# Shift and scale of the first norm as matrix products in 32-column strips, two tiles ahead of the query products

## The chip, the cores and the metric

The kernel runs on one core of a Trainium2 chip. The metric is the time of one execution on the device, in microseconds; lower is better. PE is TensorE (PEld its weight loads), DVE is VectorE, ACT is ScalarE, POOL is GpSimd, SP is SyncE, which issues most of the transfers.

## The reference

A two-part network runs on 256 tokens of width 1024: a transformer of two layers and a second block with a state-space branch, a pooling branch and 64 routed experts. The change is in the first thing that the first layer does. Two condition vectors, `c` for the tokens and `c_ctx` for 256 context tokens, go through silu and a matrix; out of the 6144 results the first 1024 are a shift, the next 1024 a scale. The normalised tokens are scaled and shifted by them, feature by feature, and then projected to queries, keys and values.

```python
def rmsnorm(x, g):
    return x * lax.rsqrt(jnp.mean(x * x, axis=-1, keepdims=True) + RMS_EPS) * g
...
silu_c, silu_cc = jax.nn.silu(c), jax.nn.silu(c_ctx)[None, :]
mod = (silu_c @ ada_w[i] + ada_b[i])[:, None, :]
mod_c = (silu_cc @ ada_w[i] + ada_b[i])[:, None, :]
sh1, sc1, g1, sh2, sc2, g2 = jnp.split(mod, 6, axis=-1)
h = rmsnorm(x, norm1_g[i]) * (1.0 + sc1) + sh1        # and hc from ctx, csh1, csc1
q, k, v = jnp.split(h @ wqkv, 3, axis=-1)             # keys and values from hc, too
```

## The kernel before

The activations lie with features on the 128 partitions: `x` is 8 tiles of 128 features by 256 tokens, and so are `ctx` (`cx`) and what is made of them. The order of every engine's instructions is the order of the Python program (`tc.manual_schedule()`); a helper inserts the semaphores.

Weights of the projections come through `Stream`: each piece `st` is 1 MB and holds two units of eight 128x128 blocks, in a ring of 4 buffers. `raw()` (L162) hands a unit over as it is, in fp32; `split_to` (L134) splits a unit into a high part `wh` (ACT, L143) and a low part `wl` (DVE, L131), which later products use in three cheaper passes (`mm3`, L274). The query products use raw units, unit n against tile n, and sum over the eight tiles in four PSUM buffers `ps_q`; so all eight tiles have to be normalised one after another, and the key products begin when the last is done.

The stage of the change runs from the start to the key products (L524 to L627). First the mean squares of `x` are formed (`sums`, L546: a square on ACT and an add on DVE per tile; `total`, L557; `row_rstd`, L565: a chain of tiny DVE operations and two products that spread the result over the partitions, `rows`). Then, for each of the eight tiles n:

- `coefs_x(n, j)` (L497): the weights of this tile's 128 shifts (j = 0) and 128 scales (j = 1) are `AW[n]`, 1 MB, with one output feature per partition. `ada_unit` (L388, L390) multiplies 1024 of its columns with `crow[:, 0]`, which is silu(c) spread over all partitions, and sums them, in one DVE operation of 128x1024.
- `coefs_c(n)` and `sum_c(n)` (L503, L508): the same for the context, by a POOL product with `crow[:, 1]` (L506) and an ACT sum (L511).
- `finish_x` (L482) and `finish_c` (L488) add bias and gain, in `ab`; `modulate` (L513) makes `na` (DVE, L516), `full` and `hH` (ACT, L519, L520) and the rest `hL` (DVE, L521).
- eight query products of 128x256 in fp32 (L617).

The program writes the coefficients of tile n+1 between the two halves of tile n's modulation, and the query products at the end of the turn. `AW` has four buffers, borrowed from `kT` and `v`; `load_a(n + 4)` (L474) reuses a buffer when its products are done. SP's queue is in program order, so a load that waits for a buffer holds the loads behind it.

In the key stage that follows, DVE also works off a background list: two products of 128x1024 with `crow` per weight unit (`ada`, L390), for the later layers' coefficients.

Of the kernel before, what the change touches and what calls it, by code (L numbers as in the profile page):

```python
# [8 lines left out]
F32 = mybir.dt.float32  # L9
# [8 lines left out]
P = 128  # L18
# [22 lines left out]
_off = 0  # L41
for _n, _w in (("ident", 128), ("tri", 128), ("cos", 256), ("sin", 256), ("pinv", 64)):
    CST[_n] = (_off, _w)
    _off += _w
NCST = _off


# [57 lines left out]
class Stream:  # L105
# [56 lines left out]
    def raw(self):  # L162

        u = self.pos // 8
        w = self.slots[u // 2][:, u % 2].rearrange("p (a c) -> p a c", a=8)
        if u % 2:
            del self.slots[u // 2]
        self.pos += 8
        self.nu = u + 1
        return w  # L170
# [249 lines left out]
def build(ctx, tc, ap):  # L420
# [14 lines left out]
    b.vecs = cp.tile([P, NVEC], F32, name="vecs")  # L435
    nc.scalar.dma_start(b.csts[:, :P], ap["csts"][:, :P])
    nc.scalar.dma_start(b.vecs[:, :VHEAD], ap["vecs"][:, :VHEAD])
# [13 lines left out]
    L0 = ExitStack()  # L451
    lp = L0.enter_context(tc.tile_pool(name="l0", bufs=1))
    qT = lp.tile([P, 8, T], F32, name="qT")
    kT = lp.tile([P, 8, 2, T], F32, name="kT")
# [19 lines left out]
    def load_a(n):  # L474
        AW[n] = spare[n % 4]
        nc.sync.dma_start(AW[n], ap["ada0s"][n])
# [16 lines left out]

    raw = cp.tile([P, KD, 4], F32, name="ada_raw")
    prods = {}
# [31 lines left out]
    st.limit = 0  # L527
    nc.sync.dma_start(crow[:, 0], ap["c"].to_broadcast([P, D]))
# [3 lines left out]
    nc.sync.dma_start(crow[:, 1], ap["c_ctx"].to_broadcast([P, D]))  # L532
    load_w()
    load_a(1)
    for i in range(2):
        nc.sync.dma_start(cxs[i], ap["ctx"][:, 4 * i:4 * i + 4])
    load_a(2)
    load_w()
    load_a(3)
    xs = [x[:, k] for k in ks]  # L540
    nc.scalar.activation(crow[:, 0], crow[:, 0], AF.Silu)
    nc.vector.scalar_tensor_tensor(bsc, b.vecs[:, ab + 8:ab + 16], 1.0, b.vecs[:, n1:n1 + 8], op0=ALU.add, op1=ALU.mult)
    ms = b.aux.tile([P, 512], F32, tag="aux", name="ms")
    rps = b.aux.tile([P, 512], F32, tag="aux", name="rows")

# [25 lines left out]

    total(0, sums(xs))
    row_rstd(0)
    coefs_x(0, 0)
    coefs_x(0, 1)
    nc.scalar.activation(crow[:, 1], crow[:, 1], AF.Silu)
    rows_x, rows_c = rps[:, :T], rps[:, T:]
    coefs_c(0)
    psq = [b.ps.tile([P, 2, T], F32, tag="ps", name="ps_q") for _ in range(4)]
    ready = []  # L580
    for n in ks:
        full = b.wk.tile([P, T], F32, tag="rp_b", name="full", bufs=2)
        todo = [modulate(xs, rows_x, n, 0, full)]
        next(todo[0])
        if n == 1:
            total(1, sums(cx))
        if n == 2:
            row_rstd(1)
        if n + 1 < KD:
            coefs_x(n + 1, 0)  # L590
        if n >= 2:
            for i in ready:
                finish_c(i)
                todo.append(modulate(cx, rows_c, i, 1))
                next(todo[-1])
            ready = []
        for o in todo:
            next(o)
        if n + 1 < KD:
            coefs_x(n + 1, 1)  # L600
        sum_c(n)
        ready.append(n)
        if n + 1 < KD:
            coefs_c(n + 1)
        if n + 4 < KD:
            load_a(n + 4)
        if n in (1, 3, 4):
            load_w()
        if n == 4:
            for t_, o in ((b.csts, "csts"), (b.vecs, "vecs")):  # L610
                c0 = P if o == "csts" else VHEAD
                nc.scalar.dma_start(t_[:, c0:], ap[o][:, c0:])
        w = st.raw()
        if n == KD - 1:
            st.more(1)
        for i in range(KD):
            nc.tensor.matmul(psq[i // 2][:, i % 2], lhsT=w[:, i], rhs=full, start=(n == 0 and i % 2 == 0), stop=(n == KD - 1),  # L617
                             skip_group_check=True)
    st.limit = st.n
    finish_c(KD - 1)  # L620
    mc_ = modulate(cx, rows_c, KD - 1, 1)
    next(mc_)
    nc.scalar.activation(qT[:, 0:2], psq[0], AF.Copy)
    next(mc_)
# [4 lines left out]
    nc.scalar.dma_start(crow[:, 1], ap["c_2"].to_broadcast([P, D]))  # L629
    b.ada_bufs = [b.adap.tile([P, D], F32, name=f"ada{i}") for i in range(2)]  # L630
# [1043 lines left out]
    ex.give(x.rearrange("p k t -> p (k t)"))  # L1674
    spare = [wr.rearrange("p k e -> p (k e)")] + [b.csts[:, P + i * T:P + (i + 1) * T] for i in range(2)]
    us = mw.tile([P, 2, 512], F32, tag="oH", name="u", bufs=1)
# [409 lines left out]
def layout(i):  # L2086
# [31 lines left out]
    o, w = CST["ident"]  # L2118
    cst[:, o:o + w] = np.eye(P)
    o, w = CST["tri"]  # L2120
    cst[:, o:o + w] = np.triu(np.ones((P, P)))
# [20 lines left out]
    out["c"] = f("c").reshape(1, D)  # L2142
    out["c_ctx"] = f("c_ctx").reshape(1, D)
    out["c_2"] = f("c_2").reshape(1, D)
    ada = f("ada_w")
    out["ada0s"] = np.ascontiguousarray(ada[0][:, :2 * D].reshape(D, 2, KD, P).transpose(2, 3, 1, 0)).reshape(KD, P, 2048)
    out["ada0"] = np.ascontiguousarray(ada[0][:, 2 * D:].T).reshape(32, P, D)
# [79 lines left out]
```

## Time and profile before

| | |
|---|---|
| median of 3 runs | 1622.66 us (1619.64 to 1630.2) |
| the profiled execution, its own time | 1618.75 us |
| its span in the profile | 1616.9 us |
| key products begin at | 84.38 us of the span |
| busy over the span: PE, DVE, ACT, POOL | 93%, 64%, 42%, 20% |

A query product in fp32 shows as two PE records, since the engine takes it in two passes; so eight of them are 16 records. A row of the timeline that joins several instructions gives the time from the first one's start to the last one's end. Records of pipelined matmuls overlap: the time that one costs is the distance to the next one's start.

### The profile page before, as it was taken

How to read it: one execution, taken by the hardware profiler on the slowest of the kernel's cores; microseconds unless marked ns; L12 is line 12 of the kernel's file. 1: busy time of each engine (PE TensorE's matmuls, PEld its weight loads, DVE VectorE, ACT ScalarE, POOL GpSimd, SP SyncE). 2: the span in 40 equal slices, each digit the busy share in tenths (PEclk: the TensorE clock that was granted, in tenths of full speed). 3: DMA queues.
4: the chain of work that ended last, by engine and by line, in shares of the span. 5: the costliest groups of instructions: out<-in, count | busy, mean ns of one | idle time of the engine just before them, and what ended most of it. 6: DMA issues, size and time to landing. Idle time of an engine off the chain costs nothing. (4 is left out here: it accounts for less than half of the span.)

```text
span 1616.9 us, 28158 instructions
## 1 busy us (share of the span) xinstructions
PE 1495.9 (93%) x11081; PEld 1200.6 (74%) x11081; DVE 1033.3 (64%) x1845; ACT 685.7 (42%) x1225; POOL 315.9 (20%) x436
## 2 busy tenths in 40 slices
PE   3699778999999899999999899999999999999996
PEld 3579558999999899999889899999644444443332
DVE  7989777887988788865878867564523332333222
ACT  4542474544445354444677665443322222222212
POOL 3644053000010200012156578001100000000000
PEclk9899998999999999999999999999999999999999
DMA  7466623888867568864344454667499799999993
GB/s 316 173 237 244 235 82 116 325 314 324 308 228 269 222 247 316 322 254 170 124 171 150 157 177 144 225 251 313 160 392 424 288 424 423 423 424 423 424 424 129
DMA packets 71862, 435.48 MB, mean 269 GB/s; under 512 B 8224, under 2 KB 8608, under 8 KB 28464
## 3 DMA queue, kind: packets, MB, share of 16 engines
q1 hardware_dynamic: 69376, 426.96, 68.9%
q0 software_dynamic: 1344, 4.80, 0.8%
q8 instruction: 88, 1.44, 0.3%
q10 hardware_dynamic: 1008, 1.89, 0.3%
q14 instruction: 46, 0.38, 0.1%
HBM read 432.55 MB, written 1.08 MB: 268 GB/s over the span
## 5 line engine op out<-in xcount | busy, mean ns | idle before, releaser
L131 DVE TENSOR_TENSOR wl<-st,wh 128x1024 fp32r<-128x1024 f32 x294 | 363.9, 1246 | 103.3 <-ACT wh L143 103.0
L143 ACT ACTIVATE wh<-st 128x1024 fp32r<-128x1024 f32 x294 | 306.7, 1056 | 126.0 <-PE ps_r L278 51.0
L277 PE MATMUL ps_f<-hh,wh 128*128 128x256 f32 x704 | 201.6, 286 | 2.5 <-ACT hh L375 2.5
L278 PE MATMUL ps_f<-hl,wh 128*128 128x256 f32 x704 | 201.5, 286 | 0.1
L279 PE MATMUL ps_f<-hh,wl 128*128 128x256 f32 x704 | 201.1, 286 | 0.0
L390 DVE SCALAR_TENSOR_TENSOR ada<-ada,crow 128x1024 f32<-128x1024 f32 x128 | 166.5, 1308 | 9.8 <-DMA ada<-in_ada 9.5
L337 POOL TENSOR_TENSOR sq<-sq 128x256 f32<-128x256 f32 x36 | 45.1, 1260 | 584.3 <-ACT sq L335 583.7
L277 PEld LDWEIGHTS ps_f<-hh,wh 128*128 128x128 f32 x704 | 137.3, 195 | 3.1 <-ACT hh L375 3.1
L278 PEld LDWEIGHTS ps_f<-hl,wh 128*128 128x128 f32 x704 | 137.2, 195 | 0.7 <-DVE hl L378 0.7
L279 PEld LDWEIGHTS ps_f<-hh,wl 128*128 128x128 f32 x704 | 137.2, 195 | 0.0
L1781 DVE TENSOR_SCALAR xb<-gtp,A,mod 128x256 f32<-128x256 f32 (+1 forms) x56 | 29.7, 530 | 126.0 <-ACT xb L1779 126.0
L277 PE MATMUL ps_ssd<-hh,wh 128*128 128x256 f32 x352 | 102.2, 290 | 0.0
L278 PE MATMUL ps_ssd<-hl,wh 128*128 128x256 f32 x352 | 99.9, 284 | 0.0
L279 PE MATMUL ps_ssd<-hh,wl 128*128 128x256 f32 x352 | 99.9, 284 | 0.0
L278 PE MATMUL ps_r<-gL,wh 128*128 128x256 f32 x352 | 99.1, 281 | 0.0
L277 PE MATMUL ps_r<-gH,wh 128*128 128x256 f32 x352 | 99.1, 281 | 0.0
L279 PE MATMUL ps_r<-gH,wl 128*128 128x256 f32 x352 | 99.0, 281 | 0.0
L1967 PE MATMUL gu<-w_y,xb 128*32 128x512 f32 (+1 forms) x352 | 92.6, 598 | 2.8 <-DMA w_y<-in_we 2.8
L1779 ACT ACTIVATE xb<-gtp,mod,A 128x256 f32<-128x256 f32 (+1 forms) x56 | 31.0, 553 | 141.5 <-PE gtp L1802 133.5
L1769 POOL TENSOR_TENSOR WG<-G,pwq 128x256 f32<-128x256 f32 (+1 forms) x24 | 14.2, 613 | 384.8 <-DVE G L1765 384.8
L1967 PE MATMUL gu<-w_st,xb 128*32 128x512 f32 (+2 forms) x376 | 83.3, 597 | 1.4 <-DMA w_st<-in_we 1.4
L271 ACT ACTIVATE oH<-wr 128x512 fp32r<-128x512 f32 (+1 forms) x53 | 33.4, 631 | 92.1 <-DVE wr L2014 92.1
(602 smaller groups left out, 4140.8 us busy)
## 6 DMA issues: line engine op xcount, KB each, us to landing
st<-in_ws SPq DMA_DIRECT2D x151, 1024.0 KB, 5.9
ada<-in_ada SPq DMA_DIRECT2D x128, 512.0 KB, 4.8
w_y<-in_we SPq DMA_DIRECT2D x48, 1024.0 KB, 17.1
w<-in_we SPq DMA_DIRECT2D x47, 1024.0 KB, 19.4
w_st<-in_we SPq DMA_DIRECT2D x38, 1024.0 KB, 19.6
w_h<-in_we SPq DMA_DIRECT2D x24, 1024.0 KB, 18.6
x<-in_we SPq DMA_DIRECT2D x11, 1024.0 KB, 17.4
w_ut<-in_we SPq DMA_DIRECT2D x8, 1024.0 KB, 19.6
```

The source lines that it names most:

```text
L131: self.b.nc.vector.tensor_tensor(lo.rearrange("p a c -> p (a c)"), w, h.rearrange("p a c -> p (a c)"), op=ALU.subtract)
L143: nc.scalar.activation(h.rearrange("p a c -> p (a c)"), w, AF.Copy)
L271: self.nc.scalar.activation(h, src, AF.Copy)
L277: nc.tensor.matmul(out, lhsT=h[:, k], rhs=xh, start=start, stop=False, skip_group_check=True)
L278: nc.tensor.matmul(out, lhsT=h[:, k], rhs=xl, start=False, stop=False, skip_group_check=True)
L279: nc.tensor.matmul(out, lhsT=lo[:, k], rhs=xh, start=False, stop=stop, skip_group_check=True)
L337: nc.gpsimd.tensor_tensor(self.acc[tag], self.acc[tag], sq, op=ALU.add)
L390: self.nc.vector.scalar_tensor_tensor(junk, w, 1.0, crow, op0=ALU.mult, op1=ALU.mult, accum_out=dst[:, j:j + 1])
L1769: nc.gpsimd.tensor_tensor(cut(WG, tt), cut(G, tt), ws_[:, tt][:, :, None].to_broadcast([P, n, c]), op=ALU.mult)
L1779: nc.scalar.activation(out[:, k, :n], tp[:, i, :n], AF.Identity, scale=A, bias=B)
L1781: nc.vector.tensor_scalar(out[:, k, :n], tp[:, i, :n], A, B, op0=ALU.mult, op1=ALU.add)
L1967: nc.tensor.matmul(gu[m:m + c], lhsT=xb[:, k, s0 + m:s0 + m + c], rhs=wt_[:, k % 4], start=(k == 0), stop=(k == KD - 1), skip_group_check= ...
```

## The change

The two condition vectors no longer lie spread over the partitions. A small array `cc` holds, for each of eight row blocks k, 32 columns of which the first two are `c` and `c_ctx` and the others zero; it is loaded into the space of `qT` and goes through silu at 128x256. The weights are laid out with the 1024 inputs on partitions and row blocks. `products(n)` computes both vectors at once on TensorE: eight products with 32 stationary columns and 256 moving columns, in fp32, where block k writes the strip of 32 PSUM partitions that begins at 32 (k mod 4), so that four strips hold partial sums. ACT copies the result to SBUF (`pa_s`), and `columns(n)` adds the strips and turns the rows into columns: two products with the 128x2 selector `sel`, written into PSUM beside the mean squares (`raw` is now a part of `ms`). The DVE products and accumulations of this stage (L390), the POOL products (L506) and the ACT sums (L511) are gone; `finish_x`, `finish_c` and `modulate` stay.

The order changes, too. The products of tiles 0 and 1 stand around the mean squares; then tile n's eight query products are cut in two halves with `products(n + 2)` between them, `columns(n + 2)` behind them, and the modulation of tile n + 1 is written after that. The context tiles follow in pairs from n = 3 on. The loads of `crow` move from the start to n = 3, on ACT's queue, and weights of the key stage are loaded and split from n = 6 on (`split_to(n + 3)`).

```diff
+    cc = qT[:, 0].rearrange("p (k c) -> p k c", k=KD)
+    nc.scalar.dma_start(cc, ap["cc"])
...
-    def coefs_x(n, j):
-        b.ada_unit(AW[n][:, j * D:(j + 1) * D], 2 * j, crow[:, 0], raw[:, n],
-                   st.hl.tile([P, D], F32, tag="wl", name="junk"))
-        if j == 1:
-            finish_x(n)
-    def coefs_c(n):
+    def products(n):
+        if n >= KD:
+            return
+        pa = b.aux.tile([P, 512], F32, tag="aux", name="pa")
+        w = AW[n].rearrange("p (k o) -> p k o", k=KD)
+        for k in ks:
+            q = 32 * (k % 4)
+            nc.tensor.matmul(pa[q:q + 32, :T], lhsT=cc[:, k], rhs=w[:, k], start=k < 4, stop=k >= 4, skip_group_check=True)
+        load_a(n + 4)
+        parts_[n] = b.wk.tile([P, T], F32, tag="sl", name="pa_s", bufs=2)
+        nc.scalar.activation(parts_[n], pa[:, :T], AF.Copy)
+    def columns(n):
+        if n >= KD:
+            return
+        p_ = parts_.pop(n)
         for j in range(2):
-            prods[n, j] = st.hl.tile([P, D], F32, tag="wl", name="prod")
-            nc.gpsimd.tensor_tensor(prods[n, j], AW[n][:, j * D:(j + 1) * D], crow[:, 1], op=ALU.mult)
-    def sum_c(n):
-        for j in range(2):
-            p_ = prods.pop((n, j))
-            nc.scalar.activation(p_, p_, AF.Copy, accum_out=raw[:, n, 2 * j + 1:2 * j + 2])
+            nc.tensor.matmul(raw[:, n, 2 * j:2 * j + 2], lhsT=p_[:, j * P:(j + 1) * P], rhs=b.cst("sel"), start=False, stop=True,
+                             skip_group_check=True)
...
+    accs_x = sums(xs)
+    products(0)
+    total(0, accs_x)
+    columns(0)
+    products(1)
     row_rstd(0)
+    columns(1)
...
+    modulate_x(0)
+    for n in ks:
+        w = st.raw()
+        for i in range(KD):
+            if i == 4:
+                products(n + 2)
+            nc.tensor.matmul(psq[i // 2][:, i % 2], lhsT=w[:, i], rhs=fulls[n], start=(n == 0 and i % 2 == 0), stop=(n == KD - 1),
+                             skip_group_check=True)
+        columns(n + 2)
         if n + 1 < KD:
+            modulate_x(n + 1)
+        if n == 1:
+            accs_c = sums(cx)
+        if n == 2:
+            total(1, accs_c)
+            row_rstd(1)
         ready.append(n)
+        if n >= 3:
+            modulate_c()
+        if n in (1, 3, 4, 5, 6):
             load_w()
...
+        if n >= KD - 2:
+            st.nu = max(st.nu, KD)
+            st.split_to(n + 3)
+    while ready:
+        modulate_c()
```

On TensorE, at the beginning of the program, the order before is this; `ms` are the mean squares, `rows` the spread result, `ps_q` the query products, `ps_k` the first key product.

```order
1 L562 MATMUL ms<-ones_73,acc 128x2 x2
2 L562 MATMUL ms<-ones_73,sq 128x2 x2
3 L569 MATMUL rows<-csts,rs_r 128x128 x2
4 L617 MATMUL ps_q<-full,st 128x256 x8
5 L562 MATMUL ms<-ones_73,acc 128x2 x2
6 L562 MATMUL ms<-ones_73,sq 128x2 x2
7 L617 MATMUL ps_q<-full,st 128x256 x8
8 L569 MATMUL rows<-csts,rs_r 128x128 x2
9 L617 MATMUL ps_q<-full,st 128x256 x48
```

And now; `pa` are the strip products of a tile's coefficients, and `ms<-csts,pa_s` the two products that turn them into columns.

```order
1 L508 MATMUL pa<-kT,qT 32x256 x8
2 L570 MATMUL ms<-ones_78,acc 128x2 x2
3 L570 MATMUL ms<-ones_78,sq 128x2 x2
4 L519 MATMUL ms<-csts,pa_s 128x2 x2
5 L508 MATMUL pa<-kT,qT 32x256 x8
6 L577 MATMUL rows<-csts,rs_r 128x128 x2
7 L519 MATMUL ms<-csts,pa_s 128x2 x2
8 L613 MATMUL ps_q<-full,st 128x256 x4
9 L508 MATMUL pa<-v,qT 32x256 x8
10 L613 MATMUL ps_q<-full,st 128x256 x4
11 L519 MATMUL ms<-csts,pa_s 128x2 x2
```

Two tiles' coefficients stand ahead of the first query product, and each later tile's stand inside the query products of the tile two before it.

On DVE, one turn in the middle of the stage stood so before; `junk` is the product and sum of 1024 columns, `hL` of two tiles, one of the tokens and one of the context.

```order
51 L390 SCALAR_TENSOR_TENSOR junk,ada_raw<-kT,crow 128x1024
52 L484 TENSOR_SCALAR ab_118<-ada_raw,vecs 128x1
53 L485 TENSOR_SCALAR ab_118<-ada_raw,vecs,bsc 128x1
54 L516 SCALAR_TENSOR_TENSOR na<-x,ab_118,rows 128x256
55 L390 SCALAR_TENSOR_TENSOR junk,ada_raw<-kT,crow 128x1024
56 L516 SCALAR_TENSOR_TENSOR na<-cx,ab_117,rows 128x256
57 L521 SCALAR_TENSOR_TENSOR hL<-na,ab_118,hH 128x256
58 L521 SCALAR_TENSOR_TENSOR hL<-na,ab_117,hH 128x256
```

The turn now, with two context tiles in it:

```order
45 L488 TENSOR_SCALAR ab_119<-ms,vecs 128x1
46 L489 TENSOR_SCALAR ab_119<-ms,vecs,bsc 128x1
47 L525 SCALAR_TENSOR_TENSOR na<-x,ab_119,rows 128x256
48 L530 SCALAR_TENSOR_TENSOR hL<-na,ab_119,hH 128x256
49 L525 SCALAR_TENSOR_TENSOR na<-cx,ab_116,rows 128x256
50 L525 SCALAR_TENSOR_TENSOR na<-cx,ab_117,rows 128x256
51 L530 SCALAR_TENSOR_TENSOR hL<-na,ab_116,hH 128x256
52 L530 SCALAR_TENSOR_TENSOR hL<-na,ab_117,hH 128x256
```

The two operations of 128x1024 are gone from every turn, and the rest of the turn is as it was.

On ACT, at the end of the stage, the order before was this; `prod` are the sums for the context, `wh` the high parts of the key weights, `qT<-ps_q` the copies of the finished queries.

```order
57 L511 ACTIVATE prod,ada_raw<-prod 128x1024 x2
58 L143 ACTIVATE wh<-st 128x1024
59 L490 ACTIVATE ab_121<-ada_raw,vecs 128x1
60 L491 ACTIVATE ab_121<-ada_raw,bsc,vecs 128x1
61 L623 ACTIVATE qT<-ps_q 128x512
62 L520 ACTIVATE hH<-na,ab_121 128x256
63 L143 ACTIVATE wh<-st 128x1024
64 L627 ACTIVATE qT<-ps_q 128x512 x3
```

And now:

```order
56 L494 ACTIVATE ab_120<-ms,vecs 128x1
57 L495 ACTIVATE ab_120<-ms,bsc,vecs 128x1
58 L529 ACTIVATE hH<-na,ab_120 128x256
59 L144 ACTIVATE wh<-st 128x1024
60 L494 ACTIVATE ab_121<-ms,vecs 128x1
61 L495 ACTIVATE ab_121<-ms,bsc,vecs 128x1
62 L529 ACTIVATE hH<-na,ab_121 128x256
63 L144 ACTIVATE wh<-st 128x1024
64 L641 ACTIVATE qT<-ps_q 128x512
65 L644 ACTIVATE qT<-ps_q 128x512 x3
```

Two units of key weights are split ahead of the first copy of queries, where one was.

## Rows read from the trace of the kernel before

**Rows 1.** Busy time by stretch: start:end, length, PE, PEld, DVE, ACT, POOL, clock, DMA, GB/s.
```profile
60.00:80.00 20.00, 12.44 (x40) 9.33 (x38) 19.89 (x29) 10.97 (x26) 13.62 (x5) 0.83 0.32 111
...
84.40:140.00 55.60, 55.07 (x287) 46.80 (x288) 52.79 (x94) 19.87 (x35) 32.88 (x21) 1.00 0.70 246
```
**Rows 2.** Waits, 0 to 84.4 us: who waited for whom, total, times, longest.
```profile
ACT full L519 <- DVE na L516: 17.3, 6, 8.8
PEld ps_q L617 <- ACT full L519: 17.1, 6, 4.2
```
**Rows 3.** Groups of instructions by line, 0 to 84.4 us: busy us, mean ns | idle before.
```profile
L617 PE MATMUL ps_q<-full,st 128*128 128x256 f32 x128 | 40.2, 483 | 14.8 <-ACT full L519 14.8
L506 POOL TENSOR_TENSOR prod<-kT,crow 128x1024 f32<-128x1024 f32 x8 | 21.2, 2658 | 21.6 <-ACT crow L576 13.8 <-DVE junk L390 5.6 <-ACT prod L511 2.2
...
L520 ACT ACTIVATE hH<-na,ab 128x256 fp32r<-128x256 f32 x15 | 7.3, 498 | 11.0 <-DVE na L516 11.0
```
**Rows 4.** Timeline of DVE, one tile's turn: start, length, instruction.
```profile
63.90 0.20 DVE L484 TENSOR_SCALAR ab<-ada_raw,vecs 128x1 f32<-128x1 f32 x1
64.02 0.26 DVE L485 TENSOR_SCALAR ab<-ada_raw,vecs,bsc 128x1 f32<-128x1 f32 x1
64.32 0.48 DVE L516 SCALAR_TENSOR_TENSOR na<-x,ab,rows 128x256 f32<-128x256 f32 x1
64.71 2.54 DVE L390 SCALAR_TENSOR_TENSOR junk<-v,crow 128x1024 f32<-128x1024 f32 x1
...
67.19 0.47 DVE L516 SCALAR_TENSOR_TENSOR na<-cx,ab,rows 128x256 f32<-128x256 f32 x1
67.58 2.80 DVE L521 SCALAR_TENSOR_TENSOR hL<-na,ab,hH 128x256 fp32r<-128x256 f32 x2
```
**Rows 5.** DMA by stretch, the columns as in rows 1.
```profile
0.00:6.00 6.00, 0.00 (x0) 0.00 (x0) 0.06 (x1) 1.49 (x2) 0.21 (x4) 1.00 0.55 175
6.00:10.00 4.00, 0.00 (x0) 0.00 (x0) 1.06 (x4) 2.61 (x6) 0.00 (x0) 1.00 1.01 371
10.00:18.00 8.00, 1.87 (x8) 1.78 (x8) 5.69 (x9) 2.61 (x5) 3.75 (x2) 1.00 1.01 423
```
**Rows 6.** Timeline from the mean squares to the first query products.
```profile
12.03 1.02 PE L562 MATMUL ms<-ones,acc 128*128 128x2 f32 x4 [12.03 <-DVE acc L554]
...
14.34 4.56 DVE L310 SCALAR_TENSOR_TENSOR rs_t<-rs_v,rs_r 128x1 f32<-128x1 f32 x2
...
19.67 1.22 PE L569 MATMUL rows<-csts,rs_r 128*128 128x128 f32 x4 [5.78 <-DVE rs_r L318]
...
23.52 6.46 PE L617 MATMUL ps_q<-full,st 128*128 128x256 f32 x16 [2.63 <-ACT full L519]
```
**Rows 7.** Timeline of PE, expert stage: strips of 32 columns and the products around them.
```profile
1400.39 0.39 PE L1802 MATMUL gtp<-G,utH 128*128 128x256 f32 x1
...
1401.32 0.28 PE L1802 MATMUL gtp<-G,utL 128*128 128x256 f32 x1
1401.53 0.62 PE L1967 MATMUL gu<-w,xb 128*32 128x512 f32 x2
1401.54 0.62 PE L1967 MATMUL gu<-w_st,xb 128*32 128x512 f32 x2
1401.98 0.60 PE L1967 MATMUL gu<-w,xb 128*32 128x512 f32 x2
```
**Rows 8.** Timeline of the third tile, and of the key products' start.
```profile
41.88 0.35 DVE L310 SCALAR_TENSOR_TENSOR rs_t<-rs_v,rs_r 128x1 f32<-128x1 f32 x2
...
43.00 0.71 PE L569 MATMUL rows<-csts,rs_r 128*128 128x128 f32 x4 [1.49 <-DVE rs_r L318]
...
43.55 3.62 PE L617 MATMUL ps_q<-full,st 128*128 128x256 f32 x16
...
84.38 0.50 PE L277 MATMUL ps_k<-hH,wh 128*128 128x512 f32 x1
...
92.19 1.22 DVE L390 SCALAR_TENSOR_TENSOR ada<-ada,crow 128x1024 f32<-128x1024 f32 x1
```

More of the change, by code (lines that the diff above doesn't have):

```diff
@@ L41 @@
 _off = 0
-for _n, _w in (("ident", 128), ("tri", 128), ("cos", 256), ("sin", 256), ("pinv", 64)):
+for _n, _w in (("ident", 128), ("sel", 2), ("tri", 128), ("cos", 256), ("sin", 256), ("pinv", 64)):
     CST[_n] = (_off, _w)
@@ L45 @@
 NCST = _off
+CHEAD = CST["tri"][0]
 S_FIX = 4
@@ L168, in raw @@
         self.pos += 8
-        self.nu = u + 1
+        self.nu = max(self.nu, u + 1)
         return w
@@ L435, in build @@
     b.vecs = cp.tile([P, NVEC], F32, name="vecs")
-    nc.scalar.dma_start(b.csts[:, :P], ap["csts"][:, :P])
+    L0 = ExitStack()
+    lp = L0.enter_context(tc.tile_pool(name="l0", bufs=1))
+    qT = lp.tile([P, 8, T], F32, name="qT")
+    cc = qT[:, 0].rearrange("p (k c) -> p k c", k=KD)
+    nc.scalar.dma_start(cc, ap["cc"])
+    nc.scalar.dma_start(b.csts[:, :CHEAD], ap["csts"][:, :CHEAD])
     nc.scalar.dma_start(b.vecs[:, :VHEAD], ap["vecs"][:, :VHEAD])
@@ L474, in load_a @@
     def load_a(n):
-        AW[n] = spare[n % 4]
-        nc.sync.dma_start(AW[n], ap["ada0s"][n])
+        if n < KD:
+            AW[n] = spare[n % 4]
+            nc.sync.dma_start(AW[n], ap["ada0s"][n])
     def load_w():
@@ L492, in finish_c @@
                              scale=b.vecs[:, n1 + n:n1 + n + 1])
-    raw = cp.tile([P, KD, 4], F32, name="ada_raw")
-    prods = {}
-    def coefs_x(n, j):
-        b.ada_unit(AW[n][:, j * D:(j + 1) * D], 2 * j, crow[:, 0], raw[:, n],
-                   st.hl.tile([P, D], F32, tag="wl", name="junk"))
-        if j == 1:
-            finish_x(n)
-    def coefs_c(n):
-        for j in range(2):
-            prods[n, j] = st.hl.tile([P, D], F32, tag="wl", name="prod")
-            nc.gpsimd.tensor_tensor(prods[n, j], AW[n][:, j * D:(j + 1) * D], crow[:, 1], op=ALU.mult)
-    def sum_c(n):
-        for j in range(2):
-            p_ = prods.pop((n, j))
-            nc.scalar.activation(p_, p_, AF.Copy, accum_out=raw[:, n, 2 * j + 1:2 * j + 2])
+    parts_ = {}
+    def products(n):
[13 more added lines that the diff above has]
+        p_ = parts_.pop(n)
+        for j in range(2):
+            nc.tensor.matmul(raw[:, n, 2 * j:2 * j + 2], lhsT=p_[:, j * P:(j + 1) * P], rhs=b.cst("sel"), start=False, stop=True,
+                             skip_group_check=True)
     def modulate(src, rows, n, i, full=None):
@@ L527, in build @@
     st.limit = 0
-    nc.sync.dma_start(crow[:, 0], ap["c"].to_broadcast([P, D]))
     for i in range(2):
@@ L531, in build @@
     load_a(0)
-    nc.sync.dma_start(crow[:, 1], ap["c_ctx"].to_broadcast([P, D]))
     load_w()
     load_a(1)
+    load_a(2)
     for i in range(2):
         nc.sync.dma_start(cxs[i], ap["ctx"][:, 4 * i:4 * i + 4])
-    load_a(2)
     load_w()
@@ L540, in build @@
     xs = [x[:, k] for k in ks]
-    nc.scalar.activation(crow[:, 0], crow[:, 0], AF.Silu)
+    nc.scalar.activation(cc, cc, AF.Silu)
     nc.vector.scalar_tensor_tensor(bsc, b.vecs[:, ab + 8:ab + 16], 1.0, b.vecs[:, n1:n1 + 8], op0=ALU.add, op1=ALU.mult)
     ms = b.aux.tile([P, 512], F32, tag="aux", name="ms")
+    raw = ms[:, 16:16 + 4 * KD].rearrange("p (n a) -> p n a", a=4)
     rps = b.aux.tile([P, 512], F32, tag="aux", name="rows")
@@ L581, in build @@
[L581 to L596, printed above, removed]
+    ready, fulls = [], {}
@@ L597, in build, with modulate_x, modulate_c @@
+    def modulate_x(n):
+        finish_x(n)
+        fulls[n] = b.wk.tile([P, T], F32, tag="rp_b", name="full", bufs=2)
+        for _ in modulate(xs, rows_x, n, 0, fulls[n]):
+            pass
+    def modulate_c():
+        todo = []
+        for i in ready[:2]:
+            finish_c(i)
+            todo.append(modulate(cx, rows_c, i, 1))
+            next(todo[-1])
+        del ready[:2]
         for o in todo:
             next(o)
-        if n + 1 < KD:
-            coefs_x(n + 1, 1)
-        sum_c(n)
@@ L608, in build @@
             load_w()
+        if n == 3:
+            nc.scalar.dma_start(crow[:, 0], ap["c"].to_broadcast([P, D]))
+            nc.scalar.dma_start(crow[:, 1], ap["c_2"].to_broadcast([P, D]))
         if n == 4:
             for t_, o in ((b.csts, "csts"), (b.vecs, "vecs")):
-                c0 = P if o == "csts" else VHEAD
+                c0 = CHEAD if o == "csts" else VHEAD
                 nc.scalar.dma_start(t_[:, c0:], ap[o][:, c0:])
-        w = st.raw()
-        if n == KD - 1:
-            st.more(1)
@@ L616, in build @@
-        for i in range(KD):
-            nc.tensor.matmul(psq[i // 2][:, i % 2], lhsT=w[:, i], rhs=full, start=(n == 0 and i % 2 == 0), stop=(n == KD - 1),
-                             skip_group_check=True)
+        if n >= KD - 2:
[3 more added lines that the diff above has]
+        modulate_c()
     st.limit = st.n
-    finish_c(KD - 1)
-    mc_ = modulate(cx, rows_c, KD - 1, 1)
-    next(mc_)
     nc.scalar.activation(qT[:, 0:2], psq[0], AF.Copy)
-    next(mc_)
@@ L628, in build @@
     st.more(3)
-    nc.scalar.dma_start(crow[:, 1], ap["c_2"].to_broadcast([P, D]))
+    nc.scalar.activation(crow[:, 0], crow[:, 0], AF.Silu)
     b.ada_bufs = [b.adap.tile([P, D], F32, name=f"ada{i}") for i in range(2)]
@@ L1674, in build @@
     ex.give(x.rearrange("p k t -> p (k t)"))
-    spare = [wr.rearrange("p k e -> p (k e)")] + [b.csts[:, P + i * T:P + (i + 1) * T] for i in range(2)]
+    spare = [wr.rearrange("p k e -> p (k e)")] + [b.csts[:, CHEAD + i * T:CHEAD + (i + 1) * T] for i in range(2)]
     us = mw.tile([P, 2, 512], F32, tag="oH", name="u", bufs=1)
@@ L2119, in layout @@
     cst[:, o:o + w] = np.eye(P)
+    o, w = CST["sel"]
+    cst[:, o:o + w] = np.arange(P)[:, None] % 32 == np.arange(2)
     o, w = CST["tri"]
@@ L2142, in layout @@
     out["c"] = f("c").reshape(1, D)
-    out["c_ctx"] = f("c_ctx").reshape(1, D)
+    out["cc"] = np.zeros((P, KD, 32), np.float32)
+    for j, n in enumerate(("c", "c_ctx")):
+        out["cc"][:, :, j] = f(n).reshape(KD, P).T
     out["c_2"] = f("c_2").reshape(1, D)
     ada = f("ada_w")
-    out["ada0s"] = np.ascontiguousarray(ada[0][:, :2 * D].reshape(D, 2, KD, P).transpose(2, 3, 1, 0)).reshape(KD, P, 2048)
+    out["ada0s"] = np.ascontiguousarray(ada[0][:, :2 * D].reshape(KD, P, 2, KD, P).transpose(3, 1, 0, 2, 4)).reshape(KD, P, 2048)
     out["ada0"] = np.ascontiguousarray(ada[0][:, 2 * D:].T).reshape(32, P, D)
```

14 lines of the change are left out of this document (removed).

## The prediction

> **What bounds the kernel now.** I read the busy time by stretch first, then the waits, the groups by line and the timeline of the first 100 us. Between 60 and 80 us DVE is busy 19.89 of 20 us, while PE has 12.44 and the DMA engines a share of 0.32 [rows 1]. The waits say the same: ACT waits for DVE's `na` for 17.3 us and PE's weight loads wait 17.1 us for ACT's `full` [rows 2]. So in the stage that ends when the key products begin, at 84.38 us [rows 8], DVE sets the pace, and what sits on it is one tile's turn of about 7.5 us [rows 4]: two products of 128x1024, of which the one beside a running POOL product takes 2.54 us, and two `hL` that take 2.80 us, again beside POOL. POOL's own products take 2.66 us each [rows 3]. The change takes both the big DVE products and all POOL products out of this stage. Behind it the picture is another: from 84.4 to 140 us PE is busy 55.07 of 55.6 us and DVE 52.79 [rows 1], so what comes out of the first stage is a shift of everything behind it.
>
> **What the change costs on TensorE.** A tile's eight query products take 3.62 us for 16 records at the higher clock (2.4 GHz) [rows 8], that is (3.62 - 0.38) / 15 = 0.216 us from record to record and 3.46 us a tile, and 6.46 us at the lower (1.2 GHz) [rows 6]. Strips are not in this stage before, but in the expert stage: four records of 32 stationary and 512 moving columns begin together, and the next four 0.45 us later [rows 7]. With 256 columns I take half, 0.225 us for four records; eight products are 16 records, so 0.9 us a tile at the higher clock and 1.8 at the lower. From below, nothing is cheaper than that; from above, strips that run one behind the other cost 16 x 0.216 = 3.5 us, or 16 x 0.39 = 6.2 us if each ran like the lone record at 1400.39 [rows 7]. I take the strip rows since they are the same kind of instruction. Going from full products to strips the trace shows 1401.53 - 1401.32 = 0.21 us where 0.12 is usual, and the first product after strips is 0.39 long instead of 0.28 [rows 7]; so a change of the array's form costs about 0.1 us each way, 0.2 a tile. The Trainium skill (TensorEngine Tiling (Array Packing), Tiling Modes) says that changing the mode drains the engine; that speaks against putting the strips between query products, and it gives no price. If a drain cost the whole 0.39 us, the six pairs would cost 4.7 us instead of 1.2; the rows show the smaller figure. The two products of `columns` are four records of 128x2 like those of the mean squares, 1.02 us at the lower clock [rows 6]; I take 0.5 us at the higher.
>
> **The start.** `crow`, 0.52 MB, no longer stands ahead of `x`; at 371 GB/s [rows 5] that is 1.4 us, so the mean squares begin at 12.03 - 1.4 = 10.6 us. By 6 us 1.05 MB have come [rows 5]; the first coefficient tile ends at 2.33 MB, so at 6 + 1.28 / 0.371 = 9.5, with 0.6 us to land 10.1. The strips then take 1.8 us (to 11.9), the mean squares 2.0 (13.9), `columns(0)` 1.0 (14.9). The second coefficient tile ends at 4.43 MB: 10 us and 2.53 MB, then 1.90 / 0.423 = 4.5 us [rows 5], landed at 15.1; strips to 16.9, `rows` 1.2 us [rows 6] to 18.1. The DVE chain beside it took 4.56 us in one pair before, next to POOL products [rows 6], against 0.35 us later [rows 8], so it is hidden behind the strips. Then `na` 0.48, `full` 0.5 and signals: query products from 19.4 us, against 23.52 [rows 6].
>
> **The stage.** 8 x 3.46 = 27.7 us for the queries, 6 x 0.9 = 5.4 for the strips of tiles 2 to 7, 6 x 0.2 = 1.2 for the changes of form, 6 x 0.5 = 3.0 for `columns`. Once, between tiles 2 and 3, PE stands: the context's mean squares (1.0), the DVE chain and its signals (2.4, since nothing else is queued between them on PE) and `rows` (0.71 [rows 8]), 4.1 us; the query products of tile 3 are behind that wait. The first tile runs at the lower clock, as it did before (6.46 against 3.62 [rows 6, 8]): 3.0 us. Sum 44.4, so the key products begin at 63.8 us and not at 84.4: 20.6 us less.
>
> **What else could be late.** On DVE a turn with two context tiles is at most 0.20 + 0.26 + 0.48 + 2 x 0.47 and three `hL`, for which 1.4 us (the pair beside POOL [rows 4]) is an upper bound: 6.1 us, and with `hL` at the price of `na` 3.3. The turn on PE is 3.46 + 0.9 + 0.2 + 0.5 = 5.1 us, and with POOL quiet the lower figure holds. On ACT a turn is `pa_s`, `full`, `hH`, two context `hH` and four tiny ones; at no more than the 498 ns of an `hH` [rows 3] that is 4.5 us, still under 5.1, but close. ACT takes in order: `pa_s` waits for the strips (2.7 us into the turn) and `full` stands behind it, so it is ready at 3.9 us, 1.2 us before PE wants it. The loads: up to the last query weights 14.9 MB must come (`x`, context, eight coefficient tiles, four weight pieces and small ones). At 423 GB/s [rows 5] that is 10 + 12.4 / 0.423 = 39 us, while tile 6, which needs the last piece, starts at 57. SP's queue waits for the strips of tiles 2 and 3 to free a buffer, with the weights behind it; those strips run by 30 us.
>
> **Behind the stage.** Two units of key weights are split before the queries end, and `wl` of the first no longer comes late. DVE's background products began 7.8 us after the key products [rows 8]; they may begin up to 2 us earlier, and DVE is nearly as full as PE there [rows 1]. Between 0 and 2 I take 1. The later order is the same, so the gain is 21.6 us.
>
> **The number.** The profiled execution took 1618.75 us by its own time (span 1616.9 and 1.85 around it); 1618.75 - 21.6 = 1597.1. The median of the runs shown, 1622.66, is 3.9 us above it. I add half of that: 1599.
>
> **Rivals.**
> 1. The strips don't overlap (other side). For it: these strips share one stationary tensor and are half as long as those in the expert stage. Against it: four records begin within 0.01 us there [rows 7]. One behind the other they cost 2.6 us more a tile in the loop, and 5.1 more for each of the two at the start, which run at the lower clock: 15.6 + 10.2 = 25.8, so 1599 + 26 = 1625. If each had to wait for the one before to finish (0.39 us a record, double at the lower clock), 32 + 21 = 53: 1652. It decides from about 3.1 us a product on, where 6 x 2.2 and 2 x 4.4 eat the gain.
> 2. The clock stays at the lower level. For it: the granted clock was 0.83 over this stage [rows 1], and a query group took 6.46 us [rows 6]. Against it: the third group, 20 us later, took 3.62 [rows 8], with PE half idle around it; now PE is denser. Then queries cost 24 us more, strips and `columns` 8, the rest 2: 1633.
> 3. The hand-over from ACT and DVE sets the turn. For it: only 1.2 us of room on ACT. If the context operations fall ahead of `pa_s`, a turn is 2 us longer in five turns: 1609. Against it: ACT's sum of 4.5 us is made with bounds.
> 4. The DMA is slower. If loads came at the 246 GB/s of the next stretch [rows 1], the last weights land at 10 + 12.4 / 0.246 = 60 us, tile 6 starts 3.5 us late: 1602. Against it: from 10 to 18 us the queue held 423 with such loads.
>
> **How the numbers follow.** About 1% (16.2 us) is what a measurement of this kernel tells from no change; faster by over 1% is below 1606.4. The forecast has 0.67, the slow DMA 0.14, and both end faster. The hand-over has 0.10, nearly all within 1%. The strips have 0.06, shared between within 1% and slower, the clock 0.03, at the edge below 1%. Faster 0.82, same 0.14, slower 0.04. The lower end takes the costs that I added and that may vanish, the lower clock at the start (3.0), PE's stand (2.4) and one more microsecond on DVE, and the profiled execution's base rather than the median's (2): 1599 - 9 = 1590. The upper end takes the hand-over and a little: 1612.
>
> **What would show it.** Right: key products near 64 us of the span; query groups about 5.1 us apart; PE busy above 0.85 from 20 us on, DVE below 0.7; strips of one tile within 1 us; one hole of some 2.5 us before tile 3. Wrong: strip records one after another; `ps_q` waiting for `full` in every turn; `pa` or `ps_q` waiting for a load; or a shift at the key products that is gone by the attention stage, where PE waits for DVE.

## The result, and the profile after

The changed kernel took 1607.95 us (median of 4 runs, 1606.16 to 1608.73) against 1625.62 for the kernel before in the same set (4 runs, 1619.64 to 1630.2): a ratio of 0.9892 [0.9854, 0.993]. Its profiled execution took 1608.24 us with a span of 1606.1, so its own time is 10.5 us under the 1618.75 of before. The prediction had 21.6 us less by that measure, and a median of 1599 us in a range of 1590 to 1612. The direction and the range held; by the profiled executions the size was off by half (the medians lie 17.7 us apart here and 12.7 in a later set with 11 runs of the kernel before), and one part of what was gained came from a place that the prediction doesn't name.

The stage of the change first. Busy time by stretch, with the columns of [rows 1]:

```profile
20.00:77.30 57.30, 45.24 (x259) 33.63 (x260) 20.84 (x64) 19.75 (x54) 0.00 (x0) 0.94 0.58 223
...
40.00:60.00 20.00, 15.64 (x88) 11.40 (x87) 6.50 (x27) 5.08 (x15) 0.00 (x0) 0.83 0.51 185
60.00:80.00 20.00, 16.47 (x88) 13.06 (x87) 10.44 (x26) 10.32 (x28) 0.00 (x0) 1.00 0.36 117
```

Where DVE was busy for 19.89 of 20 us [rows 1] it now has 10.44, and POOL has nothing. DVE is no longer the bound. But PE has only 45.24 of 57.3 us: nothing is full now, so the stage is set by a chain of waits. They are these, from the first query products to the key products (20 to 77.3 us):

```profile
DVE ab L488 <- PE ms L519: 26.1, 6, 7.3
ACT full L528 <- DVE na L525: 19.8, 8, 2.9
...
PE ps_q L613 <- ACT full L528: 9.8, 7, 1.6
```

Read from the bottom up, it is a ring: the query products wait for `full` (seven times, 9.8 us in all), `full` for `na`, and DVE's `ab`, from which `na` is made, for the products of `columns`, which stand behind the query products of the turn before. The timeline shows which columns `ab` waits for; in this stretch tile 1's query products end, tile 3's columns follow, and tile 2 is modulated:

```profile
27.74 0.50 PE L519 MATMUL ms<-csts,pa_s 128*128 128x2 f32 x4
...
29.79 1.99 PE L613 MATMUL ps_q<-full,st 128*128 128x256 f32 x8 [1.55 <-ACT full L528]
...
31.72 1.07 PE L508 MATMUL pa<-v,qT 128*32 128x256 f32 x16
...
34.55 0.50 PE L519 MATMUL ms<-csts,pa_s 128*128 128x2 f32 x4
35.09 0.22 DVE L488 TENSOR_SCALAR ab<-ms,vecs 128x1 f32<-128x1 f32 x1 [4.43 <-PE ms L519]
...
36.11 0.51 ACT L528 ACTIVATE full<-na,ab 128x256 f32<-128x256 f32 x1 [2.81 <-DVE na L525]
...
36.67 1.99 PE L613 MATMUL ps_q<-full,st 128*128 128x256 f32 x8 [1.61 <-ACT full L528]
```

The columns of tile 2 were there at 28.24 us (27.74 + 0.50). Its `ab` starts at 35.09, right behind the columns of tile 3 at 34.55, which it doesn't read. A turn, from 29.79 to 36.67, is 6.9 us and not 5.1. The key products begin at 77.34 us (63.8 predicted, 84.38 before [rows 8]), 7.0 us earlier than before. The rest of the 10.5 us comes later, and the products of the two feed-forwards (`ps_f`, one per layer) show where. The first row is of before, the second of after; for one of the three passes each gives the count, the least, median and longest duration in ns, and the first and the last start in us:

```profile
L277 PE MATMUL ps_f<-hh,wh x704: 280/283/582, 271.7 to 696.2; 128*128 128x256 f32 x176
```

```profile
L278 PE MATMUL ps_f<-hh,wh x704: 277/280/579, 264.8 to 682.2; 128*128 128x256 f32 x176
```

The first feed-forward starts 6.9 us earlier than before, the second ends 14.0 earlier: this span, with the second layer's convolution in it, is 417.4 us instead of 424.5. The 2112 feed-forward products in it take 253.8 us instead of 258.6 (from each one's start to the next one's), 4.8 of the 7.1, and the median record is 3 ns shorter. Nothing in the diff touches them. From there to the end some 3 us are lost again: the spans differ by 10.8.

### The profile page after: what moved, and what is told of

Read it like the earlier page. It is cut to its first block, busy times and chain, and to the rows that moved or that the text cites. A ratio compares the mean times of both kernels' runs of the same rounds, so it can differ in the third digit from the quotient of the medians.

```text
span 1606.1 us, 28416 instructions
## 1 busy us (share of the span) xinstructions
PE 1500.0 (93%) x11241; PEld 1197.8 (75%) x11241; DVE 986.3 (61%) x1813; ACT 670.9 (42%) x1201; POOL 268.7 (17%) x420
## 6 DMA issues: line engine op xcount, KB each, us to landing
x<-in_we SPq DMA_DIRECT2D x11, 1024.0 KB, 16.1
```

## The experiments

In what follows, the pace is the median distance from one product's start to the next, in ns, worked out from the records of a stage: before it is 229 for the key products (512 columns), 113 for the value products, 120 for the feed-forward (256 columns); after it is 235, 117 and 117. The granted clock is 1.00 in the key and value stages and 0.98 over the span of the feed-forwards, before and after. All diffs are against the changed kernel unless another is named. None of these kernels leaves out a part of the computation.

**The changed kernel again, without an edit.** Is the gain behind the stage one of this one execution?

> The changed kernel once more, nothing edited. The profiles of before and after put the key products at 84.4 and 77.3 us, 7.0 us apart, while the medians lay 17.7 us apart. If only the stage counts (theory A), the ratio is 0.993 to 0.997 and the key products begin at 77 to 78 us again; the rest is the pace of the matmuls, which was 120 ns from one to the next in the feed-forward of before and 117 ns of after, and will be another in this profile. If the change has a lasting effect behind its stage (theory B), the ratio stays at 0.985 to 0.993 and the distance at the end of the profile stays well above that at the key products.

1607.77 us (1604.54 to 1611.45, 6 runs) against 1620.46 (11 runs), ratio 0.9914 [0.9895, 0.9933]. The key products began at 77.38 us; the feed-forwards ran from 265.1 to 683.3. So it lasts: 6.6 us ahead at the start, 12.9 at the end, with paces of 235, 117 and 118. In this trace the span is 13.0 us shorter, with little lost behind the feed-forwards; what happens there differs from one execution to the next.

**The modulation of tile n+1 written ahead of `columns(n+2)`.**

```diff
-    columns(1)
...
     modulate_x(0)
+    columns(1)
     for n in ks:
...
-        columns(n + 2)
         if n + 1 < KD:
             modulate_x(n + 1)
+        columns(n + 2)
```

> modulate_x(n + 1) is written ahead of columns(n + 2) instead of behind it, at the start (tile 0 ahead of columns(1)) too; nothing else. Theory A: DVE's ab of tile n + 1 waits for the last product written into the PSUM tile ms, that of tile n + 2, and not for its own columns, so six waits of PE for full of 1.55 us and one of 0.42 us go, and with them the stretches at the lower clock: key products at 65 to 68 us instead of 77.3, PE's wait for full under 2 us in all instead of 9.4, and some 10 us less than the changed kernel in time. Theory B: the hand-over through DVE and ACT itself sets the turn (rival 3 of the prediction): the turns stay at 6.9 to 8 us and the key products at 75 us or later.

1596.29 us (1592.2 to 1600.48), ratio 0.9846 [0.9824, 0.9867]: 11.5 us less than the changed kernel of the same set. (The profiled execution, 1592.2 us, is the fastest of the five.) The same stretch of the timeline, and the start of the key products:

```profile
19.96 1.99 PE L613 MATMUL ps_q<-full,st 128*128 128x256 f32 x8 [0.51 <-ACT full L528]
...
25.08 1.97 PE L613 MATMUL ps_q<-full,st 128*128 128x256 f32 x8
26.98 1.07 PE L508 MATMUL pa<-v,qT 128*32 128x256 f32 x16
...
29.82 0.50 PE L519 MATMUL ms<-csts,pa_s 128*128 128x2 f32 x4
30.18 1.97 PE L613 MATMUL ps_q<-full,st 128*128 128x256 f32 x8
...
37.87 0.71 PE L577 MATMUL rows<-csts,rs_r 128*128 128x128 f32 x4 [1.56 <-DVE rs_r L319]
...
61.09 0.58 PE L278 MATMUL ps_k<-hH,wh 128*128 128x512 f32 x1
```

```profile
20.00:61.10 41.10, 39.16 (x261) 30.26 (x261) 20.42 (x63) 19.29 (x53) 0.00 (x0) 1.00 0.81 310
```

The turn is 30.18 - 25.08 = 5.1 us, the query products follow the columns at once, and PE is busy 39.16 of 41.1 us. The same instructions were written in another order, so the wait of `ab` is shown to be one for a product that it doesn't need. `ms` is one PSUM buffer that holds the mean squares and all tiles' columns; a reader waits for the last product that the program wrote into it ahead of the reader. Such a wait can't just be left out: the Trainium skill (PSUM — Partial Sum Buffer, "PSUM bank collisions raise a hardware error") says that two engines may not use the same bank, in the same quarter of the partitions, at one time, even at different columns; no run here shows what happens if they do. By that rule the readers have to come ahead of the next product, as here, or the columns have to alternate between banks; the second wasn't tried.

The key products begin 16.2 us earlier than after the change (77.34 to 61.09; 65 to 68 was expected), and in the profiled executions all of it arrives at the end: the spans are 16.1 us apart. The medians are only 11.5 apart; why isn't known, and the five runs spread over 8 us. The waits for `full`, 9.8 us after and 0.9 here (0.51 ahead of the first tile, 0.38 ahead of the last), make 8.9 of the 16.2. Most of the rest goes with the clock, some 5 us by adding up the products that took longer in the changed kernel. There PE began at the lower of its two levels (1.2 and 2.4 GHz) and fell back to it behind waits: the granted clock is 0.66 from 45 to 50 us and again from 55 to 60, and 1.00 here throughout. (The trace's records of the clock begin at 25.1 us in the changed kernel and at 19.3 here; ahead of them the rows give 1.00, though products there took twice as long, so the 0.94 over the changed stage is too high.) Tile 3 in the changed kernel shows it, with 3.01 us for a half group (four products) that takes 1.99 elsewhere:

```profile
45.78 1.22 PE L577 MATMUL rows<-csts,rs_r 128*128 128x128 f32 x4 [2.31 <-DVE rs_r L319]
46.80 3.01 PE L613 MATMUL ps_q<-full,st 128*128 128x256 f32 x8
```

**All eight products in one strip.** Do the four strips really run beside each other?

```diff
-            q = 32 * (k % 4)
-            nc.tensor.matmul(pa[q:q + 32, :T], ..., start=k < 4, stop=k >= 4, ...)
+            nc.tensor.matmul(pa[:32, :T], ..., start=k == 0, stop=k == KD - 1, ...)
```

(The copy and the columns then use 32 partitions.)

> All eight products of a tile write the first strip of 32 PSUM partitions, one after the other, and copy and selector take 32 partitions; the order is that of the changed kernel. Theory A (the four strips run at the same time): a tile's products take 3.5 us at the higher clock instead of 1.07 and 6.9 instead of 1.94 at the lower, so the key products begin 20 to 26 us later, at 97 to 104 us, and the kernel is slower than before. Theory B (the strips gain nothing, each product is bound by its start): the products take about as long as now, under 1.5 us, and the key products stay below 82 us.

One execution, 1625.51 us. The eight products, which took 1.07 us a tile in four strips, take 3.64:

```profile
47.52 3.64 PE L507 MATMUL pa<-kT,qT 128*32 128x256 f32 x16
...
97.35 0.58 PE L278 MATMUL ps_k<-hH,wh 128*128 128x512 f32 x1
```

The key products begin at 97.35 us, 20.0 later than after and 13.0 later than before. This is the prediction's first rival made real: it said 3.5 us a tile and 1625 us. The Trainium skill (TensorEngine Tiling (Array Packing), Theoretical Speedup) gives up to four times for operands of 32 columns or less; 3.64 / 1.07 is 3.4.

**The start mended, too.** To the order above, three edits: `bsc`, which waits for `vecs`, is written behind the adds of the mean squares; the DVE chain of `row_rstd` is written one step ahead of its products, so that PE has other work beside it; and the context tiles, which need its result, follow from n = 4 on instead of 3. The diff is against the kernel with that order.

```diff
-    nc.vector.scalar_tensor_tensor(bsc, ...)
...
     accs_x = sums(xs)
+    nc.vector.scalar_tensor_tensor(bsc, ...)
     products(0)
     total(0, accs_x)
+    r4x = rstd(0)
     columns(0)
     products(1)
-    row_rstd(0)
+    spread(0, r4x)
...
-            row_rstd(1)
+            r4c = rstd(1)
+        if n == 3:
+            spread(1, r4c)
...
-        if n >= 3:
+        if n >= 4:
             modulate_c()
```

> The order of e1_order, and two edits more: the little DVE operation bsc, which waits for vecs until 9.9 us, behind the mean squares' adds, with DVE's chain for the tokens written ahead of columns(0); and the context's rows written a tile later than its chain, so that PE doesn't stand for it. Theory A (these are plain waits in the order of PE and DVE): 2 to 3 us less at the start and 2.5 to 4 us less at tile 3 than e1_order, key products at 59 to 62 us, 15 to 18 us less than the changed kernel. Theory B (the loads of the coefficient tiles set the stage once the waits are gone): PE waits for a coefficient or a weight load instead, key products above 63 us.

1592.02 us (1587.43 to 1594.06), ratio 0.9806 [0.9786, 0.9826]. PE's stand before tile 3 is gone (from 18 to 60 us PE waits for `full` alone, 0.9 us in all). The mean squares start at 11.04 us, 2.0 earlier than in the changed kernel, as the next rows show; but the first query products, at 18.35, ran at the lower clock, which they had not in the run before:

```profile
11.04 1.02 PE L569 MATMUL ms<-ones,acc 128*128 128x2 f32 x4
...
18.35 3.78 PE L615 MATMUL ps_q<-full,st 128*128 128x256 f32 x8 [0.47 <-ACT full L528]
22.07 1.77 PE L508 MATMUL pa<-v,qT 128*32 128x256 f32 x16
```

The key products come at 60.25 us, only 0.8 earlier than with the order alone: most of what the edits gained went to the clock, whose record rises at 23.5 us here and at 19.3 in the run before. The medians are 4.3 us apart, but the intervals of the two ratios touch, so that these edits are worth anything isn't shown.

**PE kept busy from the start.** Five products of zeros, 128x512, are added ahead of the mean squares (extra work, into `rps`), on top of the run before.

```diff
+    idle = qT[:, 1:3].rearrange("p a t -> p (a t)")
+    nc.gpsimd.memset(idle, 0.0)
+    for _ in range(5):
+        nc.tensor.matmul(rps, lhsT=idle[:, :P], rhs=idle, ...)
     accs_x = sums(xs)
```

> e5_all with five fp32 products of zeros, 128x512, on TensorE from the first microsecond, while it waits for the loads; their result is overwritten. In e5_all the strips and small products before 18 us and the first half of the query products of tile 0 ran at the lower clock (1.94 us for a tile's strips, 3.78 us for four query products against 1.97). Theory A (what the engine did before decides the clock): strips of tile 0 in 1.07 us, query products of tile 0 from about 16.5 us instead of 18.35 and at the higher clock, key products 3 to 5 us earlier than 60.25, so 55 to 57.5 us. Theory B (the start is bound by loads, or the clock doesn't follow): key products at 59 us or later.

1595.05 us (1589.77 to 1598.11), ratio 0.9844 [0.9821, 0.9866]; key products at 59.80. No gain is shown (without these products the ratio is 0.9806 [0.9786, 0.9826]):

```profile
1.32 6.58 PE L583 MATMUL rows<-qT 128*128 128x512 f32 x10 [1.32 <-POOL qT L581]
9.40 1.07 PE L508 MATMUL pa<-kT,qT 128*32 128x256 f32 x16 [1.50 <-DMA kT<-in_ada0s]
...
14.31 1.94 PE L508 MATMUL pa<-kT,qT 128*32 128x256 f32 x16 [1.97 <-DMA kT<-in_ada0s]
...
18.51 3.78 PE L619 MATMUL ps_q<-full,st 128*128 128x256 f32 x8 [0.47 <-ACT full L528]
```

The first strips ran at the higher level (1.07 us instead of 1.94). But the granted clock, 1.00 up to 12.2 us, is 0.50 from 12.4 to 22.4: it fell just as PE began to wait, for 1.97 us, for the second coefficient tile, and the strips of that tile and the first query products behind it are at the lower level again. At the start the load is the limit, which the prediction had put at 15.1 us and which came at 14.3.

**The kernel before, again.** The runs from here on ask why the feed-forwards got faster. The changed kernel's constants grew by `sel`, 32 bytes with its padding, and a tile of 128 bytes (`ada_raw`) is gone, so the activations behind them (`hH`, `hL`, and `hh`, `hl` of the feed-forwards) lie 96 bytes lower. Theory L says that the pace hangs on the addresses, theory C that it hangs on the execution or on what went before.

> The kernel before, once more, for its paces: theory L expects 229, 113 and 120 ns again; theory C lets them be others, 117 ns in the feed-forward among them.

One execution, 1621.85 us. The paces are 229, 117 and 120. The feed-forwards' and the key products' are those of before; the value products' is not (117 instead of 113), with the same addresses: a miss for theory L in that stage.

**The kernel before, with its buffers 96 bytes lower.** Against the kernel before:

```diff
-(("ident", 128), ("tri", 128), ...
+(("ident", 128), ("gap", 2), ("tri", 128), ...
...
-    raw = cp.tile([P, KD, 4], F32, name="ada_raw")
+    raw = mods[2][:, :4 * KD].rearrange("p (n a) -> p n a", a=4)
```

> The kernel before, with two unused columns in csts and the sums ada_raw kept in the still unused mods[2], and nothing else: every tile behind the constants then lies 96 bytes lower in SBUF, as in the changed kernel. Theory L (the address of the operands sets the pace of the matmuls): the pace of the changed kernel comes with it, 117 ns instead of 113 in the value products, 235 instead of 229 in the key products, 117 to 119 instead of 120 in the feed-forward, and with that 4 to 8 us less than before in all, although the first stage still ends at 84 us. Theory C (the pace depends on the run or on what went before): paces of 229, 113 and 120 ns as before, and a ratio of 0.998 to 1.002.

1615.74 us (1610.45 to 1621.12, 12 runs) against 1619.72 (17 runs): 0.997 [0.9955, 0.9984].

```profile
L277 PE MATMUL ps_f<-hh,wh x704: 277/281/579, 273.0 to 691.6; 128*128 128x256 f32 x176
```

The stage of the change is the old one (key products at 85.59), but the feed-forwards span 418.6 us and not 424.5, and the paces are 232, 117 and 118. (The profiled execution, at 1620.79 us the second slowest of the twelve, loses its lead between 760 and 980 us, where its granted clock is 0.95 and that of before 0.99.)

**The changed kernel, with its buffers where they were.**

```diff
     bsc = cp.tile([P, KD], F32, name="bsc")
+    cp.tile([P, 24], F32, name="gap")
```

> The changed kernel with an unused tile of 96 bytes a partition behind bsc, so that the tiles behind the constants lie where they lay before. Theory L: paces of 229 and 113 ns in key and value products and 120 ns in the feed-forward; the stage's gain of 7 us stays, 2 to 3 us come with the key and value products, and the 6 to 7 us of the feed-forward are lost: 1611 to 1614 us. Theory C: paces and time of the changed kernel, 1606 to 1609 us.

1611.05 us (1607.47 to 1616.58, 6 runs), ratio 0.9933 [0.9915, 0.9952].

```profile
L278 PE MATMUL ps_f<-hh,wh x704: 278/283/582, 262.2 to 685.8; 128*128 128x256 f32 x176
```

The feed-forwards are back at 423.6 us, and the paces are 229, 113 and 120, those of before. (By the kernels' memory plans the split weights `wh` and `wl` lie elsewhere in the changed kernel, and this edit leaves them there; so it is not they.) The two runs agree: 0.9933 x 0.997 = 0.990, and the whole change measured 0.9914 [0.9895, 0.9933]. So of the gain some 0.7% is the new stage, and some 0.3% comes from where the buffers lie: 3 to 7 us by the interval of the kernel before with its buffers moved, about 3 by the medians of this run and the changed kernel, whose intervals overlap. The span of the feed-forwards shows it without overlap: 423.6 to 424.5 us in the three traces with the addresses of before, 417.3 to 420.4 in the seven with 96 bytes less. (This run's profiled execution, at 1616.58 us the slowest of its six, loses some 8 us of its lead between 760 and 980 us, where its granted clock is 0.96.)

**The mended kernel, 32 and 64 bytes higher.** Is it the address modulo 64 bytes that counts? In both, the kernel with the mended start has an unused tile, of 8 or of 16 columns, behind `bsc`.

> e5_all with an unused tile of 32 bytes a partition behind bsc, so that the tiles behind the constants lie 64 bytes below those of the kernel before (e5_all: 96 below). If only the address modulo 64 bytes counts, the paces are those of the kernel before: 229 ns in the key products, 113 in the value products, 120 in the feed-forward, and the time is 2 to 5 us above that of e5_all. If the pace repeats over a longer stretch, they are others; then the time lies within 5 us of e5_all on either side.

> e5_all with an unused tile of 64 bytes, so that the tiles lie 32 bytes below those of the kernel before. If only the address modulo 64 bytes counts, the paces are those of e5_all (235, 117, and 117 to 120 ns) and the time is the same within 2 us. If the pace repeats over a longer stretch, they are others.

With 32 bytes: 1588.43 us (1581.54 to 1589.89), ratio 0.9795 [0.9774, 0.9816], paces 227, 120 and 118, a third pattern. By the address modulo 64 they should have been those of the kernel before. With 64 bytes: 1596.42 us (1595.27 to 1599.33, 4 runs), ratio 0.9859 [0.9839, 0.9879], paces 234, 117 and 117; these are as expected, but the time was to be within 2 us of the run without the tile (1592.02), and it is 4.4 above. Modulo 64 is not the rule. The first row below is the kernel with 32 bytes, the second that with 64:

```profile
L278 PE MATMUL ps_f<-hh,wh x704: 276/281/583, 248.7 to 665.7; 128*128 128x256 f32 x176
```

```profile
L278 PE MATMUL ps_f<-hh,wh x704: 277/281/582, 247.3 to 668.8; 128*128 128x256 f32 x176
```

The spans are 417.0 and 421.5 us, and 420.4 without the tile. Nor is one address one pace: without the tile the feed-forwards' is 120 where the changed kernel, with the same addresses, has 117, and in the kernel before with moved buffers it is 119 in the first feed-forward and 117 in the second. What rule sets the pace stays open. The kernel with 32 bytes is the best that was measured, some 31 us under the 1619.62 of before in its set; of that, the change has 12.7 (1620.46 less 1607.77) and the order 11.5; the last 7 are the start and the addresses, which these runs don't separate.

## Why the prediction was right and wrong

- **DVE as the bound: right.** DVE is at 10.44 of 20 us where it had 19.89 [rows 1], and POOL has nothing from 20 us on.
- **The prices on TensorE: right.** Strips at 0.9 us a tile and 0.2 for the change of form: one tile's strips span 1.07 us, and the next query products begin 1.00 behind the strips' start. Cold strips 1.8: 1.94. Columns 0.5: 0.50. Strips that run one behind the other 3.5: 3.64, shown by the run with one strip. The stand before tile 3, 2.4 us for the chain: 2.31 (1.56 with the order mended). With the order mended the turn is the predicted 5.1 us, and the stage from the first query products to the key products takes 41.1 us; the predicted 44.4 had 3.0 for a first tile at the lower clock, which that run didn't have.
- **"`full` stands behind it, so it is ready at 3.9 us, 1.2 us before PE wants it": the step that failed.** It counted each engine's work and the queue on ACT, and followed the strips to `pa_s`, but not `ab`, which has to read the same PSUM buffer that the next columns are written to. `ab` of tile n+1 starts behind the columns of tile n+2, and these come last in the turn; so `ab`, `na` and `full` lie behind the turn and not beside it. From the first query products to the key products it took 56.3 us (77.34 - 21.0) where 44.4 were predicted: 8.2 of the 11.9 too many are the six waits for `full` behind the first (9.8 less the 1.55 ahead of 21.0), and most of the rest goes with the lower clock, which is read from rows and not from a run of its own. That the order is the cause is shown by the run that changes it alone. `ps_q` waiting for `full` in every turn is a sign of being wrong that the prediction itself names.
- **The start: off by 1.6 us.** Query products at 21.0 us, not 19.4. 1.0 of it is the failed step again, for tile 0's `ab` waits for `columns(1)`: with the order alone mended they begin at 19.96. And the mean squares began at 13.06 and not at 10.6:

```profile
9.86 0.17 DVE L549 SCALAR_TENSOR_TENSOR bsc<-vecs 128x8 f32<-128x8 f32 x1 [8.98 <-DMA vecs<-in_vecs]
9.94 3.07 DVE L562 TENSOR_TENSOR acc<-acc,sq 128x256 f32<-128x256 f32 x6
...
13.06 1.01 PE L570 MATMUL ms<-ones,acc 128*128 128x2 f32 x4 [1.70 <-DVE acc L562]
```

  `bsc` stands ahead of the adds on DVE and waits for `vecs` until 9.86 us; the step took `x` for the only load that the adds wait for. The run that moves `bsc` starts the mean squares at 11.04.
- **"+1 behind the stage": wrong, and small.** DVE's first `ada` product comes 8.5 us behind the key products (85.82), not earlier than the 7.8 of before [rows 8]. What was gained at the key products (7.0 us) is still there at the first feed-forward's start (6.9), so the argument that the shift carries through holds.
- **The DMA: right.** In the loop no product waits for a load.
- **What the sum didn't have.** The matmul pace moved with the buffers, which the diff's first lines (`sel`) and the lost tile `ada_raw` bring about; 3 to 7 us by the run of the kernel before with its buffers moved. Without it the changed kernel is at 1611, at the upper end of the range: that the median fell well inside is in part luck.
- **The rivals.** The hand-over as the bound (1609) came nearest, 0.10 by the prediction: right in its sign, in PE's waits for `full` and in its size, but with another cause, since it put the delay on ACT's order. The strips do overlap. The clock did not stay at the lower level, but came back to it in stretches (0.83 from 40 to 60 us). Faster by over 1%, which had 0.82, is at the edge: 1.1% in this set and 0.9 in the next.

## What to carry to other kernels

Where a loop writes the next tile's results into the PSUM buffer from which this tile's are read, write the readers ahead of that product in program order: here this moved the key products by 16 us and the median by 11.5, with the same instructions. Before an engine's room in a turn is counted as room, follow the chain through every shared buffer and ask which write the reader waits for, not only which it needs. And where a change moves constants or small tiles, compare the pace of stages that it doesn't touch before the whole difference is put down to the edit.

## What the runs showed of the hardware

- At a granted clock of 1.00, the value products (256 columns) follow each other at a median of 113 to 120 ns and the key products (512 columns) at 227 to 235, in kernels whose buffers are shifted by multiples of 32 bytes; the feed-forwards' products, at 0.98, at 117 to 120. The value products had 113 and 117 in two executions of one kernel. The Trainium skill (TensorE: Matmul & The Clock Gate, "Wait — 56ns, not 53.3ns?") gives the columns by the clock plus a fixed 2.5 ns; for 256 columns that would be 109 ns, an estimate by that page, and no stage here reaches it; over the columns by the clock (107 and 213 ns) the stages have 6 to 13 ns more at 256 columns and 14 to 22 at 512.
- Keeping PE busy at the start doesn't by itself hold the clock: after 6.58 us of products and the first tile at the higher level, the granted clock went from 1.00 to 0.50 at 12.3 us, as a wait of 1.97 us began, and the strips behind it ran at the lower level. The same first query products ran at the higher level in one kernel (1.99 us for eight records, behind a wait of 0.51) and at the lower in another (3.78, behind 0.47): the records of the clock rise at 19.3 us in the one and at 23.5 in the other, and what decided that isn't seen.
